# One order and one buffer table in place of another, in a hybrid encoder layer on one core

## The chip, the cores and the metric

The kernel runs on one core of a Trainium2 chip. The metric is the device time of one execution in microseconds; the median of three executions is compared. The core has five engines with a queue each: TensorE (PE, with its weight loads shown apart as PEld), VectorE (DVE), ScalarE (ACT), GpSimd (POOL) and SyncE (SP), which only issues DMAs. SP, ACT and POOL each can start DMAs. An engine does its queue in order; engines wait for one another by semaphores.

## The reference

One layer takes x (1 x 512 x 1024, float32) through a mixing step and a feed-forward step:

```python
h = rmsnorm(x, mix_norm[l])
p = h @ w_in[l]                      # 1024 x 9248: rx, ry, qkv, z, ba, gates
y_rnn = rglru_branch(rx, ry, ...) @ w_rnn_proj[l]
y_dn = deltanet_branch(qkv, z, ba, ...) @ w_dn_proj[l]
g_rnn, g_dn = jnp.split(jax.nn.sigmoid(gates), 2, axis=-1)
x = x + (g_rnn * y_rnn + g_dn * y_dn) @ w_out[l]
gt, up = jnp.split(rmsnorm(x, ffn_norm[l]) @ w_gate_up[l], 2, axis=-1)
x = x + (jax.nn.silu(gt) * up) @ w_down[l]
```

The DeltaNet branch has 8 heads, each run forwards and backwards over the sequence in chunks of 64. Within a chunk a triangular system is solved; from chunk to chunk a 128 x 128 state S is carried, and this recurrence is serial:

```python
def step(S, inp):
    v_new = u_c - w_c @ S
    o = qg_c @ S + att_c @ v_new
    S = S * exp(gl_c) + kd_c.T @ v_new
```

## The kernel before

**Stages.** x is normalised and transposed into `hh` and `hl`, its high and low parts for TensorE; a float32 product is made of three matmuls of such parts (`mm3`, L806), and the large weight matrices go through blocks of seven products in place of eight (`products` L1327, `merged` L1289, `gate_up` L1772). In order of time: the projections and the 12 blocks of the recurrent branch (`rg_front` L913, `rg_out` L951); the z products and the gate products; four DeltaNet groups of two heads each (`dn_front` L970, `dn_mats` L1014, `dn_inverse` L1051, `dn_state` L1135, `dn_out` L1214); the output projection; 22 blocks of gate and up, and down.

**The groups.** A group's `dn_mats` writes a tile `na` of which there is one, so groups follow each other. While a group runs, the z and gate products and the next group's front stand between its instructions, on TensorE above all: they are the only other work there, and the text calls them filler.

**The recurrence.** `dn_state` (L1135) works on four chains at once (two directions, two heads), in four steps, each of which takes two of the reference's chunks. Each chain owns 128 of the 512 columns of a tile. Cut to the chain of work:

```python
for ch in chains:                                                   # L1151
    T.matmul(pks[:, sl4[ch]], kq[...], st[:, sl4[ch]], ...)
for ch in chains:                                                   # L1157
    V.scalar_tensor_tensor(rhs[:, sl4[ch]], pks[:, sl4[ch]], negc[...], vn[...], ...)
for ch in chains: T.matmul(py[:, sl4[ch]], Y[...], rhs[:, sl4[ch]], ...)
A.copy(ys, py)
for ch in chains: T.matmul(pu[:, sl4[ch]], kd[:, sl4[ch]], ys[:, sl4[ch]], ...)
for ch in chains:                                                   # L1183
    V.scalar_tensor_tensor(nst[:, sl4[ch]], st[:, sl4[ch]], egl[...], pu[:, sl4[ch]], ...)
```

`kd` is made by GpSimd ahead of time. In step 0 `pks` is left out and ScalarE copies `pu`; the last step leaves out `pu`. Beside the chain, `pq` (the state with q) and `pi` (the attention with `ys`) take four matmuls each, and small operations of VectorE and ScalarE add them into the output `o`. Where a matmul writes into a PSUM tile and another engine reads any slice of that tile, the one waits for the other if it stands behind it: the dependence is kept for the tile, not for the slice.

**What sets the order.** The functions don't run their operations; `Rec` (L514) records each of them, 9344 in all, with its engine and the tiles it names. `Plan.emit` (L491) then issues them by the table `ORDER` (L31), a permutation of their numbers that was written out beforehand. So every instruction in a profile has line L525, the line in `Rec` that records it, and is told apart by its tiles. A second table, `HOMES` (L430), gives every tile of three pools (`t2`, of 512 columns, `t4`, of 1024, and `ps`, the eight PSUM banks) the buffer it lies in. A tile's first writer waits for the last users of the buffer's tile before; `Plan.emit` adds those waits.

**The start.** SP loads x in four pieces and the first weights in halves; GpSimd loads the small parameters (conv weights, biases, lambda and the norm's gain) as rows of one tile, `prow` (L719 to L733), which TensorE turns into `par`. GpSimd also does eight subtractions that split the first weights into parts.

Of the kernel before, what the change touches and what calls it, by code (L numbers as in the profile page):

```python
# [31 lines left out]
2 1686 0 1 5 6 12 14 4 1685 140 3 10 11 13 1703 7 153 152 151 17 18 19 20 21 66 67 145 142 141 5682 146 144 22 23 24  # L32
25 26 27 28 29 30 31 32 57 1704 1689 49 15 1687 65 35 33 70 43 16 143 41 71 1690 1688 1724 34 37 36 39 68 69 72 38
1705 42 73 75 40 74 59 1723 154 147 45 46 44 77 51 1707 47 97 9 58 50 60 1691 1692 1693 1697 1698 1699 1700 1701
1702 48 76 78 79 88 81 80 1706 1708 84 93 1741 85 364 1694 1742 92 52 155 55 56 1725 1727 148 53 104 1743 61 54 1726
1728 89 105 106 96 1744 1745 1715 1716 1695 1696 1709 1710 1711 1717 1718 1719 1720 1729 1730 1735 312 62 63 1712
107 1731 1736 149 150 1737 1713 1714 1721 94 64 203 98 1732 1733 86 99 1738 1739 1740 1753 1754 1755 125 95 82 1734
1747 1748 1749 117 234 100 101 909 87 90 1111 102 103 111 390 135 83 1746 1750 1751 1756 1757 1758 133 158 636 127
91 313 1752 126 134 235 124 128 109 285 363 108 1759 130 119 118 236 286 156 110 132 112 665 114 131 315 910 113 122
115 753 1080 129 1722 116 314 316 317 318 319 320 120 136 418 391 159 121 1763 883 321 322 137 855 237 754 1764 138  # L40
123 1765 582 756 1112 139 238 239 240 241 392 323 757 160 1113 762 767 1760 1761 417 324 325 326 327 528 242 243 244
245 246 247 248 249 250 251 252 253 254 255 256 257 258 259 260 261 262 263 264 265 666 328 329 330 287 393 394 331
332 333 334 335 336 337 338 339 340 341 342 343 344 345 346 637 347 348 349 350 351 352 353 354 355 356 357 358 359
360 361 362 367 266 267 268 269 270 271 272 273 274 275 276 277 278 279 280 281 282 283 284 289 368 4823 290 161 162
163 164 758 760 474 365 369 291 288 205 165 166 167 168 169 170 370 1021 292 171 172 173 174 175 176 177 178 179 180
181 182 183 184 185 186 187 188 189 190 191 192 1081 856 395 396 397 398 193 195 583 197 638 196 194 198 199 157 371
293 294 399 419 1235 400 401 402 403 404 405 406 407 858 408 409 420 410 411 412 413 414 415 1766 416 882 303 216
859 529 200 366 204 759 860 206 861 531 532 857 421 207 295 422 299 300 208 307 423 304 305 862 863 381 301 372 382
308 209 309 296 297 864 302 377 424 425 584 210 306 383 426 378 379 384 1762 212 865 1022 866 439 440 211 755 441
213 530 373 374 375 380 310 777 214 427 376 867 8 215 778 992 1173 780 311 442 298 428 431 432 429 433 434 435 436  # L50
437 763 438 385 386 387 388 781 761 218 533 534 535 536 430 786 791 219 782 783 1236 1237 784 764 868 869 870 884
785 389 475 537 538 539 1174 443 871 872 873 874 875 876 877 878 879 880 881 449 1114 451 1082 540 541 542 543 544
886 768 770 444 477 1115 772 545 546 547 548 549 887 779 888 453 765 217 501 885 550 551 552 553 554 559 4822 452
454 911 445 1116 792 794 936 560 448 1117 476 796 1118 1119 450 462 561 889 1083 1084 1085 1086 1087 1088 1089 1090
1091 1092 1175 787 789 1093 1094 1095 1096 1097 1098 1099 1100 1101 1102 1103 1104 788 790 562 468 456 502 769 771
1120 1121 1122 1123 1124 1125 1126 1127 1128 1129 1130 1131 1132 1133 1134 1135 1136 1137 1138 555 556 609 610 766
585 586 587 588 589 590 591 592 593 594 595 596 597 598 599 600 601 602 463 1139 1238 1239 1240 478 446 890 900 904
464 1140 1141 563 1105 1106 447 455 896 603 892 891 897 905 604 605 1107 898 1241 1242 901 793 899 1055 902 564 906
907 893 894 895 1054 1068 1243 469 606 607 608 613 1244 479 480 481 482 483 484 485 486 1024 466 1108 1023 829 465
557 201 1025 487 488 489 490 491 492 493 494 495 496 497 498 499 500 1109 1056 457 1110 558 1057 1245 1246 1247 1248  # L60
1249 614 615 616 565 505 506 507 569 1026 1027 1028 797 798 1250 1251 1252 1253 1254 1255 1256 508 566 570 1257 1258
611 612 567 617 631 618 619 1069 1259 1260 1261 1029 1030 1266 632 993 571 572 509 202 458 667 1031 1032 1033 568
937 620 621 1034 1035 1036 470 1037 573 574 575 1038 503 577 578 579 1039 576 903 580 622 510 1040 1041 1042 1043
1044 623 624 459 1045 801 802 625 626 1046 994 511 1047 504 731 633 803 732 1346 523 515 4788 512 513 514 467 516
517 518 728 471 627 628 629 630 938 634 472 1262 912 913 581 724 726 635 524 730 727 734 795 460 1373 1176 1177 1263
908 1070 723 939 1071 828 914 915 916 917 1178 1179 1264 725 1265 995 996 918 919 920 921 922 923 924 925 926 927
928 929 930 931 932 933 934 935 940 941 942 943 963 525 729 733 804 805 806 747 807 808 809 810 811 812 813 814 815
816 817 818 819 748 820 821 822 823 824 825 826 827 1180 1181 1182 1183 1184 1185 1186 1187 1188 1189 1190 1191 832
833 834 835 1192 1142 741 1193 1194 461 1072 735 997 1195 800 1073 4838 4856 4824 998 999 1000 1001 944 945 1002
1003 773 775 742 519 520 521 1269 668 4839 1004 1005 1006 1007 1008 1009 1010 1011 1012 958 946 1013 1048 1014 1015  # L70
947 954 749 959 1143 743 522 1204 960 736 4789 774 1196 1197 1198 1199 1200 1016 1017 1018 961 4804 955 956 745 639
744 830 831 957 962 526 1454 836 837 1374 1201 669 670 671 672 673 674 675 676 677 678 679 680 681 682 683 684 950
1455 527 951 952 776 1656 685 1205 953 948 949 1059 1058 1061 1202 640 641 1145 686 687 688 689 690 691 1144 964
1203 737 738 739 842 473 1019 1401 1206 642 643 644 645 1400 692 646 647 648 649 650 651 652 653 654 655 656 657 658
659 660 661 662 663 846 847 850 843 838 848 1281 849 751 220 844 222 224 839 840 841 851 852 853 845 1273 740 1319
1481 1279 1207 1208 1209 1210 1051 1280 694 746 750 854 4840 1050 1060 1146 1211 1212 1213 1214 1215 1216 1217 1218
1219 1220 1221 1222 1053 4805 1223 1224 1225 1226 1227 1228 1229 1230 1231 1052 1147 1148 1149 1150 1151 1152 1153
1154 4825 4841 693 1427 664 1074 1285 966 967 968 969 1272 1375 965 228 227 229 1232 1233 1270 695 696 1155 1156
1234 1062 1157 1158 1159 1160 1161 1162 1163 1164 1165 1166 1167 1168 1169 1170 970 971 972 973 232 231 233 1271
1274 223 221 974 975 976 977 978 979 980 981 982 983 1320 984 1171 985 986 987 4861 988 989 1347 1268 1172 4895 1267  # L80
1275 752 4857 1321 1322 1283 1323 990 1020 1063 1456 1298 1049 1276 230 2374 2400 2375 2379 2378 2377 1075 1287 1296
2401 1299 1303 1402 1300 1324 1325 1326 1327 1328 1329 1330 1331 1332 1333 1334 2376 1335 1336 1376 1377 1282 1378
1337 1076 1077 225 1403 1286 1338 1339 1340 1064 1066 1341 1348 1342 1343 1344 1277 1284 1345 1302 1379 1380 1381
1382 1383 1384 1385 1386 1387 1388 1389 1390 1391 1392 1393 1394 1395 1396 1350 1351 1352 4790 1065 1397 1398 1399
1278 2367 2368 2370 2371 2369 1404 1405 1428 2372 1406 1407 4806 697 698 699 700 701 702 703 704 1353 705 706 707
708 709 710 711 712 713 714 715 716 717 1657 718 719 1408 720 4791 1430 991 1431 4874 4875 721 1297 1414 1418 1409
1410 1411 1412 4807 1415 1419 1420 1354 1422 1423 1413 2373 1424 1416 4934 1301 1421 1355 1067 4792 4793 4794 4795
4796 4797 4798 4799 4800 4801 1572 1429 1417 1573 4878 4947 1425 1078 1432 1433 1434 1435 1436 1437 1438 1439 1440
1441 1442 1443 1444 1586 1445 1446 1447 2393 1448 1449 1450 722 1457 1451 1452 4876 4877 1453 1458 4802 4803 4814
# [1925 lines left out]
```

## Time and profile before

| | |
|---|---|
| median of three executions | 1127.9 us (1127.46 to 1131.09) |
| the profiled execution | 1131.04 us, its span 1129.3 us |
| PE busy | 1068.6 us, 95% |
| VectorE, ScalarE, GpSimd busy | 956.8, 764.9 and 118.8 us |
| mean PE clock granted | 0.975 |
| moved by DMA | 186.31 MB, 165 GB/s |

The span runs from the first to the last instruction that the profiler saw; the execution's time holds 1.7 us beside it. Names of tiles stand without their numbers in the profile: `ps` is any PSUM tile, `t` any tile of `t2` and `t4`, `negc`, `ge` and `par` constant tiles. An entry such as "PE ps <- DVE t: 8.7, 15, 1.8" says that PE was idle for 8.7 us, 15 times and at most 1.8 us, before instructions that write `ps`, until VectorE had written a `t`; what VectorE read before that isn't in it.

### The profile page before, as it was taken

The numbers are of one execution on the slowest core, as the hardware profiler recorded it, in microseconds if no ns is written. First come the engines' busy times: TensorE is split into PE (matmuls) and PEld (weight loads), VectorE is DVE, ScalarE is ACT, GpSimd is POOL, SyncE is SP. The second block draws the span as 40 slices with busy tenths as digits, with TensorE's granted clock in tenths as the row PEclk, the third lists the DMA queues.
The fourth block names the chain that finished last, engine by engine and source line by source line (L and its number), as shares of the span: only waits on it lengthen the run. The fifth ranks groups of instructions, "written<-read, shape, count | busy, mean of one in ns | idle before, by whom it ended". The sixth has DMA issues, their size and how long they took to land.

```text
span 1129.3 us, 18175 instructions
## 1 busy us (share of the span) xinstructions
PE 1068.6 (95%) x6623; PEld 913.1 (81%) x6623; DVE 956.8 (85%) x1707; ACT 764.9 (68%) x1397; POOL 118.8 (11%) x165
## 2 busy tenths in 40 slices
PE   7899999999999889988988898899999999999997
PEld 6887888878888668767866676788999999998786
DVE  4899999888798679847984884799989989999997
ACT  5899999974766457867986465468745554555674
POOL 5000001220302222121222000000000000000000
PEclk8999999999999999989988998999999999999999
DMA  9742472896569869964954550485154556435632
GB/s 281 199 136 91 140 190 65 198 230 180 155 182 204 180 210 259 247 150 134 236 136 92 141 177 20 168 261 178 57 169 150 162 173 202 135 109 172 214 140 75
DMA packets 170874, 186.31 MB, mean 165 GB/s; under 512 B 8704, under 2 KB 120464, under 8 KB 170784
## 3 DMA queue, kind: packets, MB, share of 16 engines
q1 hardware_dynamic: 157648, 156.43, 44.8%
q0 software_dynamic: 11808, 25.30, 13.2%
q10 hardware_dynamic: 1328, 3.42, 0.8%
q8 instruction: 52, 0.85, 0.3%
q14 instruction: 38, 0.31, 0.1%
HBM read 159.92 MB, written 18.91 MB: 158 GB/s over the span
## 4 chain that ended last, share of the span: by engine, by line
PE 72%; DVE 12%; ACT 10%; issue 3%; DMA 2%; SPq 0%; ACTq 0%; DVEq 0%
PE ps L525 72%; DVE t L525 11%; ACT t L525 7%; ACT L525 1%; DVE na L525 1%; DMA osums<-t 1%; DMA t<-in_w_in_dram 1%; ACT na L525 0%; DMA sums<-t 0%; ACT ps L525 0%; DMA t<-in_w_gate_up_dram 0%; ACT hh L525 0%; ACT rst L525 0%; SPq L525 0%; ACTq L525 0%
## 5 line engine op out<-in xcount | busy, mean ns | idle before, releaser
L525 PE MATMUL ps<-t,t 128*128 128x512 f32 (+3 forms) x3195 | 599.4, 334 | 27.5 <-DVE t L525 20.2
L525 DVE TENSOR_TENSOR t<-t,t 128x512 fp32r<-128x512 f32 (+15 forms) x839 | 553.0, 686 | 58.5 <-ACT t L525 28.2
L525 PEld LDWEIGHTS ps<-t,t 128*128 128x128 f32 (+1 forms) x3195 | 465.1, 182 | 106.4 <-DVE t L525 32.9
L525 ACT CAST t<-t 128x512 fp32r<-128x512 f32 (+2 forms) x418 | 323.0, 809 | 156.5 <-DVE t L525 66.8
L525 PE MATMUL ps<-hh,t 128*128 128x512 f32 (+2 forms) x1424 | 375.8, 341 | 0.8 <-DVE na L525 0.8
L525 PEld LDWEIGHTS ps<-hh,t 128*128 128x128 f32 (+1 forms) x1424 | 249.6, 190 | 32.4 <-ACT t L525 2.0
L525 PE MATMUL ps<-hl,t 128*128 128x512 f32 (+2 forms) x720 | 232.7, 340 | 0.0
L525 PEld LDWEIGHTS ps<-hl,t 128*128 128x128 f32 (+1 forms) x720 | 135.5, 190 | 14.0
L525 ACT COPY t<-ps 128x256 f32<-128x256 f32 (+3 forms) x168 | 70.1, 434 | 92.4 <-PE ps L525 84.9
L525 ACT ACT_TABLE_LOAD x69 | 88.5, 1283 | 4.1 <-DVE t L525 1.8
L525 DVE SCALAR_TENSOR_TENSOR t<-ps,par,t 128x511 f32<-128x511 f32 (+1 forms) x108 | 79.3, 745 | 6.5 <-ACT t L525 4.9
L525 ACT ACTIVATE t<-t 128x512 f32<-128x512 f32 (+5 forms) x118 | 72.1, 618 | 12.9 <-DVE t L525 12.2
L525 DVE TENSOR_TENSOR t<-ps,t 128x256 f32<-128x256 f32 (+1 forms) x102 | 53.3, 530 | 17.2 <-PE ps L525 14.7
L525 PE MATMUL ps<-t,na 128*128 128x128 f32 (+2 forms) x640 | 56.3, 241 | 9.8 <-DVE t L525 7.1
L525 PEld LDWEIGHTS ps<-t,na 128*128 128x128 f32 (+2 forms) x640 | 48.4, 151 | 18.3 <-DVE t L525 10.3
L525 PE MATMUL ps<-ident,t 128*128 128x128 f32 (+2 forms) x232 | 44.5, 284 | 10.6 <-DVE t L525 3.9
L525 DVE TENSOR_TENSOR t<-t 128x512 f32<-128x512 f32 (+1 forms) x84 | 53.2, 639 | 1.4 <-DMA t<-in_w_down_dram 0.8
L525 ACT ACTIVATE t<-ps,par 128x512 f32<-128x512 f32 x68 | 45.6, 710 | 7.1 <-PE ps L525 6.9
L525 POOL DMA_DIRECT2D t<-in_w_in_dram x24 | 29.8, 1303 | 194.1 <-PE ps L525 110.2
L525 PEld LDWEIGHTS ps<-ident,t 128*128 128x128 f32 (+2 forms) x232 | 30.1, 146 | 19.9 <-DVE t L525 5.7
L525 POOL TENSOR_SCALAR_AFFINE_SELECT t<-t 128x512 f32<-128x512 f32 x32 | 24.9, 787 | 138.0 <-DMA t<-gcr 85.0
L525 DVE SCALAR_TENSOR_TENSOR t<-ps,negc,t 128x128 f32<-128x128 f32 x48 | 16.4, 349 | 25.3 <-PE ps L525 25.1
(153 smaller groups left out, 700.8 us busy)
## 6 DMA issues: line engine op xcount, KB each, us to landing
t<-in_w_in_dram SPq DMA_DIRECT2D x66, 512.0 KB, 5.5
t<-in_w_gate_up_dram SPq DMA_DIRECT2D x44, 512.0 KB, 4.6
t<-in_w_in_dram POOLq DMA_DIRECT2D x24, 512.0 KB, 7.5
t<-xqd SPq DMA_DIRECT2D x48, 256.0 KB, 4.0
t<-in_w_down_dram SPq DMA_DIRECT2D x22, 512.0 KB, 3.9
t<-in_w_down_dram SPq DMA_DIRECT2D x33, 256.0 KB, 4.1
t<-in_w_in_dram SPq DMA_DIRECT2D x24, 256.0 KB, 4.6
t<-t POOLq DMA_DIRECT2D x12, 512.0 KB, 6.0
```

The costliest lines, as they stand in the source:

```text
L525: self.plan.ops.append((self.eng, {x.tensor.name for x in aps}, outs, lambda: real(*a, **kw)))
```

## The change

The code is the same in both kernels from L473 on, and so are the operations. The two tables are new: `ORDER` issues the same 9344 operations in another sequence, and `HOMES` deals the buffers out anew. A line or two of the tables, since their rows say nothing by themselves:

```diff
 ORDER = """
-2 1686 0 1 5 6 12 14 4 1685 140 3 10 11 13 1703 7 153 152 151 17 18 19 20 21 66 67 145 142 141 5682 146 144 22 23 24
...
```

What it does is seen in the engines' queues. Three places follow.

**PE, step 1 of the recurrence of the last group.** `ps1167` is `pks` (its matmuls take the state t21165), t21168 is `rhs`, `ps1169` is `py`; `ps945`, `ps946`, `ps1016` and `ps1166` belong to filler, transposes and the output of step 0. Before:

```order
L525 MATMUL ps1167_1244<-t21165_1242,t41033_1110 128x128 [waits Activation_49]
L525 MATMUL ps1167_1244<-t21165_1242,t41020_1097 128x128
L525 MATMUL ps945_1022<-t4951_1028,t4932_1009 128x512
L525 MATMUL ps946_1023<-t4951_1028,t4931_1008 128x512
L525 MATMUL ps1167_1244<-t21165_1242,t41033_1110 128x128 [waits DVE_49]
L525 MATMUL ps1167_1244<-t21165_1242,t41020_1097 128x128 [waits DVE_49]
L525 MATMUL ps1166_1243<-t21162_1239,na1136_1213 128x128 [waits Activation_49]
L525 MATMUL ps1169_1246<-t21168_1245,na1136_1213 128x128 x2
L525 MATMUL ps1169_1246<-t21168_1245,na1136_1213 128x128 [waits DVE_49]
```

With the change:

```order
L525 MATMUL ps1167_1244<-t21165_1242,t41033_1110 128x128 [waits Activation_49]
L525 MATMUL ps1167_1244<-t21165_1242,t41033_1110 128x128
L525 MATMUL ps1167_1244<-t21165_1242,t41020_1097 128x128 x2
L525 MATMUL ps1016_1093<-ident1_78,t4979_1056 128x128
L525 MATMUL ps945_1022<-t4951_1028,t4931_1008 128x512
L525 MATMUL ps1166_1243<-t21162_1239,na1136_1213 128x128 [waits Activation_49]
L525 MATMUL ps945_1022<-t4952_1029,t4931_1008 128x512
L525 MATMUL ps1169_1246<-t21168_1245,na1136_1213 128x128 [waits DVE_49] x4
```

The third and fourth matmul of `pks` each waited for VectorE; now the four stand together with one wait, and a transpose and two 512-column matmuls stand behind them, ahead of `py`.

**VectorE, the same step.** t21173 is `nst`, the new state, and ps1172 is `pu`. Before:

```order
L525 SCALAR_TENSOR_TENSOR t21168_1245<-ps1167_1244,negc97_174,t41019_1096 128x128
L525 TENSOR_SCALAR nq1053_1130<-nq1053_1130 128x8
L525 SCALAR_TENSOR_TENSOR t21168_1245<-ps1167_1244,negc97_174,t41019_1096 128x128 x3
L525 TENSOR_TENSOR t41273_1350<-t41269_1346,t41272_1349 128x1024
L525 TENSOR_TENSOR t41218_1295<-t41216_1293,t41217_1294 128x1024
L525 SCALAR_TENSOR_TENSOR t21173_1250<-t21165_1242,ge96_173,ps1172_1249 128x128 x3
```

With the change:

```order
L525 SCALAR_TENSOR_TENSOR t21168_1245<-ps1167_1244,negc97_174,t41019_1096 128x128 x4
L525 TENSOR_TENSOR t4105_182<-t4105_182,t21067_1144 128x512
L525 TENSOR_TENSOR t41273_1350<-t41269_1346,t41272_1349 128x1024
L525 SCALAR_TENSOR_TENSOR t21173_1250<-t21165_1242,ge96_173,ps1172_1249 128x128 x3
L525 SCALAR_TENSOR_TENSOR t21177_1254<-ps1176_1253,negc97_174,t41019_1096 128x128 x2
```

The reads stand in one piece; between `rhs` and `nst` stand two other operations of VectorE, as before.

**GpSimd, the start.** t266 is `prow`, and the TENSOR_TENSOR rows are the eight subtractions. Before:

```order
L525 DMA t266_143<-in_dn_norm_dram 1x16x8
L525 DMA t266_143<-in_rg_conv_b_dram 12x128
L525 DMA t266_143<-in_rg_conv_w_dram 48x128
L525 DMA t266_143<-in_dn_conv_w_dram 96x128
L525 DMA t266_143<-in_rg_bx_dram 24x128
L525 DMA t266_143<-in_rg_ba_dram 24x128
L525 TENSOR_TENSOR t4454_531<-t4452_529,t4453_530 128x512 x2
L525 DMA t266_143<-in_rg_lambda_dram 24x128
```

With the change:

```order
L525 DMA t266_143<-in_rg_ba_dram 24x128
L525 TENSOR_TENSOR t4454_531<-t4452_529,t4453_530 128x512 x2
L525 TENSOR_TENSOR t4457_534<-t4455_532,t4456_533 128x512 x2
L525 TENSOR_TENSOR t4462_539<-t4460_537,t4461_538 128x512 x2
L525 TENSOR_TENSOR t4465_542<-t4463_540,t4464_541 128x512 x2
L525 MEMSET zero_t70_147 128x1
L525 DMA t266_143<-in_rg_bx_dram 24x128
L525 AFFINE_SELECT sl5_82<-ones6_83 128x128
L525 DMA t266_143<-in_rg_lambda_dram 24x128
```

All but one of the parameter loads have moved behind the eight subtractions. On SP the first two weight halves now stand ahead of the first piece of x, and the small weights of `ba` come earlier.

875 rows, old and new, of tables (HOMES, ORDER) are left out of this document.

## The prediction

> **What bounds the kernel now.** I read the page first, for the engine that ends last. The rows are the span, the busy times, and PE's busy tenths and clock in 40 slices of 28.2 us.
>
> ```profile
> span 1129.3 us, 18175 instructions
> PE 1068.6 (95%) x6623; PEld 913.1 (81%) x6623; DVE 956.8 (85%) x1707; ACT 764.9 (68%) x1397; POOL 118.8 (11%) x165
> PE   7899999999999889988988898899999999999997
> PEclk8999999999999999989988998999999999999999
> ```
>
> TensorE is the bound, and what can be won without taking matmuls away is small: 1129.3 - 1068.6 = 60.7 us of idle, and the cycles that the throttle withheld. The eights stand in slices 14-15, 18-19, 21-23 and 25-26, so I cut the span there, at the stages of the DeltaNet groups (columns: window, its length, busy time of PE, PEld, DVE, ACT, POOL with counts, PE clock, DMA share, GB/s).
>
> ```profile
> core 0: us, PE busy (x) PEld busy (x) DVE busy (x) ACT busy (x) POOL busy (x), PEclk, DMA share, GB/s
> 0.00:56.00 56.00, 46.37 (x267) 40.74 (x268) 37.34 (x76) 37.96 (x72) 17.19 (x29) 0.91 0.85 239
> 56.00:357.00 301.00, 299.85 (x1528) 243.00 (x1527) 273.47 (x388) 254.94 (x377) 38.92 (x41) 1.00 0.61 159
> 357.00:417.50 60.50, 51.65 (x280) 42.34 (x279) 40.09 (x78) 32.24 (x73) 11.78 (x15) 1.00 0.75 185
> 491.00:535.00 44.00, 37.61 (x215) 31.96 (x215) 29.59 (x65) 29.17 (x67) 7.59 (x18) 0.92 0.43 122
> 577.00:595.80 18.80, 16.13 (x246) 12.81 (x247) 13.04 (x24) 12.51 (x27) 5.53 (x5) 0.74 0.66 148
> 595.80:636.00 40.20, 30.94 (x187) 24.66 (x186) 22.92 (x64) 19.39 (x44) 6.08 (x14) 0.95 0.44 99
> 681.20:718.20 37.00, 29.52 (x166) 23.78 (x166) 20.41 (x52) 17.26 (x44) 0.00 (x0) 0.90 0.11 36
> 745.00:1129.30 384.30, 374.13 (x2542) 346.04 (x2540) 358.10 (x577) 227.51 (x419) 0.00 (x0) 0.99 0.49 155
> ```
>
> From 56 to 357 us PE idles 1.15 us of 301, and from 745 on 10.2 of 384: nothing is to be had there. The four recurrences (`dn_state`, at 357, 491, 596 and 681 us) idle 8.85 + 6.39 + 9.26 + 7.48 = 32.0 us, the start 9.6. In the recurrences no engine is full: in the last one PE stands at 80%, DVE at 55%, ACT at 47%, DMA at 0.11. That is a chain of short steps. What ends PE's waits: first the whole span, then the windows 374 to 417.5, 491 to 535, 595.8 to 636 and 681.2 to 718.2 in that order (columns: us, times, longest).
>
> ```profile
> PEld ps L525 <- DVE t L525: 49.4, 76, 3.2
> PE ps L525 <- DVE t L525: 31.2, 52, 2.9
> ...
> PE ps L525 <- DVE t L525: 8.7, 15, 1.8
> ...
> PE ps L525 <- DVE t L525: 5.7, 10, 1.4
> ...
> PE ps L525 <- DVE t L525: 3.1, 7, 0.7
> ...
> PE ps L525 <- DVE t L525: 7.3, 15, 1.1
> ```
>
> Of PE's 31.2 us of waits on a VectorE result, 8.7 + 5.7 + 3.1 + 7.3 = 24.8 us, in 47 waits (0.53 us each), lie in the four recurrences. What such a wait is, the timeline at 496 us shows (start, duration, work, and in brackets the idle time before it and who ended it).
>
> ```profile
> 496.14 0.35 DVE L525 SCALAR_TENSOR_TENSOR t<-ps,negc,t 128x128 f32<-128x128 f32 x1 [0.25 <-PE ps L525]
> 496.55 0.49 PE L525 MATMUL ps<-t,t 128*128 128x128 f32 x2 [0.44 <-DVE t L525]
> ...
> 497.08 0.35 DVE L525 SCALAR_TENSOR_TENSOR t<-ps,negc,t 128x128 f32<-128x128 f32 x1 [0.58 <-PE ps L525]
> ...
> 498.01 0.35 DVE L525 SCALAR_TENSOR_TENSOR t<-ps,negc,t 128x128 f32<-128x128 f32 x1 [0.58 <-PE ps L525]
> ...
> 498.94 0.35 DVE L525 SCALAR_TENSOR_TENSOR t<-ps,negc,t 128x128 f32<-128x128 f32 x1 [0.58 <-PE ps L525]
> ```
>
> The four matmuls of `pks` go into four slices of one PSUM tile, each read by one scalar_tensor_tensor into `rhs`. They need nothing of each other. Yet matmul and read alternate, 0.93 us from read to read: the next matmul starts only when the read of the slice before has ended, since that read stands ahead of it in the table and the dependence is kept for the tile as a whole. The same kernel, at step 3 of group 2, also has the other order, and beside it PE's pace where nothing waits.
>
> ```profile
> 618.41 0.61 PE L525 MATMUL ps<-t,t 128*128 128x128 f32 x4
> ...
> 618.86 0.83 PE L525 MATMUL ps<-t,na 128*128 128x128 f32 x6
> ...
> 621.36 0.61 PE L525 MATMUL ps<-t,t 128*128 128x128 f32 x4
> ...
> 622.08 0.35 DVE L525 SCALAR_TENSOR_TENSOR t<-ps,negc,t 128x128 f32<-128x128 f32 x1 [1.08 <-PE ps L525]
> ...
> 622.80 0.86 DVE L525 SCALAR_TENSOR_TENSOR t<-ps,negc,t 128x128 f32<-128x128 f32 x3
> ```
>
> Four matmuls in a row start 0.11 us apart (618.41 to 618.86). First matmul to last read is 622.80 + 0.86 - 621.36 = 2.30 us here. In the alternating form it is the 0.53 us from matmul to read (496.55 to 497.08) and the reads' 498.94 + 0.35 - 496.14 = 3.15, together 3.68. Three alternations cost 1.38 us, 0.46 each.
>
> **The change, step by step.** I counted, in both orders, the places where a matmul into a tile of `dn_state` comes behind a read of another slice of it.
>
> *`pks` and `pu`*, which are the chain: 46 such places before (by group 15, 12, 6 and 13), 13 after (3, 4, 2 and 4). 33 x 0.46 = 15.2 us. Bounds: above, a read at full pace costs 0.86 / 3 = 0.29 of the 0.93, so 33 x 0.64 = 21.1; below, half is covered by matmuls of other stages that fill the gap already, 7.6.
>
> *`pi` and `pq`*, the outputs: 34 places before, 20 after. Nobody on the chain waits for them, but their matmuls hold PE's queue. 14 x 0.53 = 7.4 at most, 0 at least; I take half, 3.7.
>
> *Filler.* Of the 32.0 us of idle, 32.0 - 24.8 = 7.2 are waits for something else (ScalarE's copy of `py`, the tile `na`). The new order puts a 512-column matmul or a transpose at most of these places. Half, 3.6; bounds 0 and 7.2.
>
> *`dn_inverse`, `dn_mats`, `merged`.* The same count falls from 5 to 1 in the inverse, and rises from 4 to 8 in `dn_mats` and from 13 to 17 in the gate products: -4 + 8 = 4 waits more, 4 x 0.53 = 2.1 us lost; bounds 0 and 4.2.
>
> *Clock.* In the three later windows it was 0.92, 0.95 and 0.90. Their busy times at full clock would be shorter by 37.61 x 0.08 + 30.94 x 0.05 + 29.52 x 0.10 = 7.5 us. Half, 3.8; bounds 0 and 7.5. [...]
>
> *The start.* x's loads, the first half weights and GpSimd's queue change places.
>
> ```profile
> 3.66 0.53 POOL L525 DMA_DIRECT2D t<-in_rg_conv_w_dram  x1
> ...
> 5.74 1.28 POOL L525 TENSOR_TENSOR t<-t,t 128x512 fp32r<-128x512 f32 x1
> ...
> 8.25 0.77 PE L525 MATMUL ps<-ident,t 128*128 128x128 f32 x5 [0.85 <-DMA t<-in_x_dram]
> ...
> 13.46 0.90 PE L525 MATMUL ps<-ident,t 128*128 128x128 f32 x3 [2.94 <-DVE t L525]
> ```
>
> The wait of 2.94 us at 13.46 is again a transpose behind a read of its own tile, and there are 3 such places in `raw_transpose` before, none after; the wait for x is 0.85. Together 3.8, less what the parameters may cost. GpSimd issued six of their loads (0.53 each) ahead of its eight subtracts (1.28 each); now one stands ahead and the rest behind, so the last is issued at least 8 x 1.28 + 7 x 0.53 = 14 us after the first subtract. The first convolution needs them, and PE has matmuls of the first products until then, so I set it at 0, at most 7 (the seven issues, 3.7, and about as long again to land). The start: 3.8, bounds -3 and 7.
>
> The weight loads on SP (390 queue rows now, 396 before) are dealt out anew as well; I take 0, and the rival below is about that. **Sum:** 15.2 + 3.7 + 3.6 - 2.1 + 3.8 + 3.8 = 28.0 us. Against the profiled execution's own time, 1131.0 us (span 1129.3 and 1.7 around it), that is 1103.0. This execution was 3.1 us above the median of the three shown (1127.9), and the wait pattern I price repeats in every execution: 1127.9 - 28.0 = 1099.9. By a second way, the last recurrence alone: its work at full pace, from these rows of 681.2 to 718.2 us and a full stretch of 512-column work,
>
> ```profile
> L525 PE MATMUL ps<-t,t 128*128 128x128 f32 x72 | 14.1, 306 | 5.9 <-DVE t L525 5.9
> L525 PE MATMUL ps<-t,na 128*128 128x128 f32 x64 | 12.3, 320 | 1.6 <-DVE t L525 1.4
> L525 PE MATMUL ps<-t,t 128*128 128x512 f32 x22 | 10.6, 518 | 0.0
> L525 PE MATMUL ps<-ident,t 128*128 128x128 f32 x8 | 2.0, 355 | 0.0
> ...
> 56.47:84.70 28.23, 28.23 (x127) 23.28 (x126) 27.98 (x47) 28.07 (x43) 0.00 (x0) 1.00 0.44 136
> ```
>
> is 144 x 0.11 + 22 x 0.22 = 20.7 us in a window of 37.0. So 16.3 us are lost in this one, more than twice its idle time of 7.48, because "busy" holds each lone matmul's latency. This makes me lean to the larger side of the first term: I forecast **1099 us**.
>
> The orders of PE and VectorE at this recurrence's step 1 show that the places counted are really gone for `pks`, and one is left in `pu`.
>
> **Rivals.** *Full recovery.* The chain falls below PE's work in all four groups, and PE's own pace sets the stage. Then all 24.8 + 7.2 = 32.0 us of idle and 7.5 of clock go, and the start's 7: 1127.9 - 46.5 = 1081.4, say 1083. For it: 16.3 of 37.0 us lost in the last group. Against: each step still has py, ScalarE's copy and pu in series, and 13 + 20 places are left.
>
> *The stall only moves.* `py` needs the reads, ScalarE's copy needs all of `py`, and what is saved at `pks` is waited for at `pu`. Then the lower bounds hold: 7.6 + 0 + 0 - 2.1 + 0 + 3.8 = 9.3, 1118.6. For it: the first read now comes 0.72 us after the first matmul (621.36 to 622.08) where it came 0.53 after. Against: reads are done 1.38 us sooner in the pair of rows above.
>
> *Slower: weights late in the full stretches.* The place is SP's queue, in order, with the loads
>
> ```profile
> t<-in_w_in_dram SPq DMA_DIRECT2D x66, 512.0 KB, 5.5
> t<-in_w_gate_up_dram SPq DMA_DIRECT2D x44, 512.0 KB, 4.6
> ```
>
> A load into a buffer still in use blocks all loads behind it, and both tables, order and buffers, are new. PE has 1.15 us of slack in 56 to 357 us, and VectorE is at 91% there; so lateness goes straight into the end. These 110 loads turn the gain of 28 around from 0.25 us of mean lateness each; at 0.3 us it is 33 us, 1133. Against: the buffers let the loads run ahead by more than their 5 us today, or PE would idle more than 1.15 us in a stretch of 301.
>
> *It does not do what it says:* other stages' matmuls cover the waits that go, and the time stays at 1128. Against it stand the 24.8 us, which are PE's own idle time.
>
> **How the numbers follow.** The forecast's case has 0.56, with 1088 to 1112 as its own range (the clock, the filler and half of the first term either way); full recovery 0.20; the moved stall 0.14; late weights 0.06; no effect 0.04. The range 1080 to 1120 takes in the first three. A change of this kernel can be told from none at about 0.3%, 3.4 us: faster 0.56 + 0.20 + 0.14 = 0.90, within it 0.04, slower 0.06.
>
> **What would show it.** Right: in the four recurrences the matmul-read alternation at 0.93 us is gone from the timeline, PE's waits on VectorE there fall from 24.8 us to under 12, and their windows shrink by 4 to 9 us each, while 56 to 357 and the end keep their lengths. Wrong: the windows shrink but waits on ScalarE's copy or on `na` take their place (the moved stall); PE waits for a weight load anywhere in the full stretches; the first convolution waits for GpSimd's parameters at 25 to 35 us. A clock still at 0.90 with fewer waits would show that term wrong.

## The result, and the profile after

The changed kernel takes 1064.3 us (median of four, 1061.3 to 1065.7), the kernel before beside it 1128.3: a ratio of 0.9425, with a 95% interval of 0.9398 to 0.9451. The direction was forecast; the size was not. 64 us were won where 28 were forecast, and 1064.3 lies below the range's 1080.

The page of the changed kernel, the same rows as were shown of the kernel before:

```profile
span 1062.0 us, 18192 instructions
PE 1037.3 (98%) x6623; PEld 897.1 (84%) x6623; DVE 948.1 (89%) x1707; ACT 758.2 (71%) x1392; POOL 124.9 (12%) x165
PE   8899999999999999999999999999999999999997
PEclk9999999999999999989999999999999999999999
```

The span is shorter by 67.3 us. PE's idle time fell from 60.7 to 24.7, by 36.0; PE's busy time fell by 31.3, with the same 6623 matmuls. That second half is what the forecast's sum hardly had in it. The mean clock rose from 0.975 to 0.994: what the throttle withheld fell from 1129.3 x 0.025 = 28.2 us to 1062.0 x 0.006 = 6.4, a bound of 21.8 us for its share. Single executions of the kernel before read from 0.973 to 0.989 in the later sets, mostly 0.98, so 16 us is the more usual share.

The stages, now the whole span (columns as in the table of windows before), the recurrences at 351, 476, 562 and 631 us:

```profile
core 0: us, PE busy (x) PEld busy (x) DVE busy (x) ACT busy (x) POOL busy (x), PEclk, DMA share, GB/s
0.00:62.00 62.00, 53.80 (x315) 46.76 (x316) 47.41 (x93) 47.78 (x86) 21.12 (x29) 0.97 0.88 250
62.00:351.00 289.00, 287.49 (x1471) 233.44 (x1470) 257.85 (x365) 239.00 (x355) 35.67 (x39) 1.00 0.60 158
351.00:402.00 51.00, 50.16 (x291) 43.17 (x290) 43.04 (x84) 35.11 (x73) 11.42 (x10) 1.00 0.87 207
402.00:476.50 74.50, 71.64 (x507) 57.94 (x506) 60.68 (x129) 56.31 (x120) 26.06 (x36) 0.97 0.98 259
476.50:507.50 31.00, 31.00 (x210) 27.96 (x209) 26.19 (x63) 26.70 (x65) 5.34 (x13) 0.97 0.45 118
507.50:562.50 55.00, 53.63 (x435) 42.77 (x433) 52.71 (x136) 48.14 (x109) 15.91 (x19) 1.00 0.86 221
562.50:591.00 28.50, 28.09 (x200) 25.29 (x201) 24.71 (x67) 20.24 (x47) 7.08 (x15) 1.00 0.68 157
591.00:631.00 40.00, 39.41 (x366) 32.02 (x366) 37.26 (x107) 30.13 (x62) 2.30 (x4) 1.00 0.61 185
631.00:651.50 20.50, 20.50 (x159) 19.12 (x159) 16.08 (x42) 14.24 (x33) 0.00 (x0) 1.00 0.15 48
651.50:1062.00 410.50, 401.58 (x2685) 368.62 (x2683) 382.21 (x630) 240.58 (x450) 0.00 (x0) 1.00 0.52 162
```

The stages of the kernel before that the prediction's table does not show:

```profile
417.50:491.00 73.50, 71.26 (x507) 57.03 (x506) 59.67 (x130) 54.62 (x115) 19.60 (x28) 0.95 0.98 253
535.00:577.00 42.00, 40.52 (x183) 32.55 (x182) 39.64 (x109) 39.53 (x85) 9.84 (x12) 1.00 0.81 205
636.00:681.20 45.20, 44.17 (x380) 36.29 (x379) 37.71 (x106) 27.96 (x62) 2.31 (x4) 0.93 0.55 158
718.20:745.00 26.80, 26.42 (x137) 21.93 (x136) 24.78 (x46) 11.78 (x20) 0.00 (x0) 1.00 0.72 233
```

In the four recurrences PE now idles 0.84 + 0 + 0.41 + 0 = 1.3 us, where it idled 32.0. The last one has gone from 37.0 us to 20.5 with about as many matmul records (166 and 159). At the prediction's pace these are now 142 x 0.11 + 17 x 0.22 = 19.4 us of work.

The windows of the recurrences shrank by 9.5, 13.0, 11.7 and 16.5 us, 50.7 together, where the prediction expected 4 to 9 each. Only 30.7 of this is idle time. The other 20.0 is PE's busy time, which fell from 149.7 to 129.7 us there with 848 and 860 matmul records. The stretch ahead of the first recurrence is 6.0 us shorter (351 against 357, with 1786 and 1795 matmul records), the stretches between the recurrences lost 10.0 us together (179.5 to 169.5), and what follows the last one 0.6 (411.1 to 410.5). So 16.6 us of the 67.3 were won outside the recurrences.

PE's waits in the whole span:

```profile
PE ps L525 <- ACT t L525: 7.9, 13, 1.3
PEld ps L525 <- DVE t L525: 7.4, 19, 0.8
PE ps L525 <- DMA dtb<-in_dn_dt_bias_dram: 4.3, 1, 4.3
PE ps L525 <- DVE t L525: 1.4, 4, 0.5
```

PE's waits on a VectorE result were 31.2 us in 52; now they are 1.4 in 4. There is one new wait, of 4.3 us at the start. Step 1 of the last recurrence in the timeline shows what a step has become:

```profile
635.17 1.15 PE L525 MATMUL ps<-t,t 128*128 128x128 f32 x8
...
636.19 0.47 PE L525 MATMUL ps<-t,t 128*128 128x512 f32 x1
...
636.36 1.13 DVE L525 SCALAR_TENSOR_TENSOR t<-ps,negc,t 128x128 f32<-128x128 f32 x4
...
636.64 0.48 PE L525 MATMUL ps<-t,t 128*128 128x512 f32 x1
...
636.96 1.07 PE L525 MATMUL ps<-t,na 128*128 128x128 f32 x8
```

A float32 matmul of 128 columns stands in the trace as two, so x8 are the four of `pks`. They take 1.15 us, the four reads run in one piece of 1.13 right behind, and under them PE has filler, without a bracket of idle time anywhere, until `py` at 636.96; the last read ends at 636.36 + 1.13 = 637.49.

### The profile page after: what moved, and what is told of

It is laid out like the page before. It is cut to its first block, busy times and chain, and to the rows that moved or that the text cites. A ratio compares the mean times of both kernels' runs of the same rounds, so it can differ in the third digit from the quotient of the medians.

```text
span 1062.0 us, 18192 instructions
## 1 busy us (share of the span) xinstructions
PE 1037.3 (98%) x6623; PEld 897.1 (84%) x6623; DVE 948.1 (89%) x1707; ACT 758.2 (71%) x1392; POOL 124.9 (12%) x165
## 5 line engine op out<-in xcount | busy, mean ns | idle before, releaser
L525 DVE TENSOR_TENSOR t<-t,t 128x512 fp32r<-128x512 f32 (+18 forms) x839 | 551.4, 684 | 47.4 <-ACT t L525 30.0
L525 PE MATMUL ps<-t,t 128*128 128x512 f32 (+3 forms) x3195 | 575.1, 329 | 4.4 <-ACT t L525 3.4
L525 PEld LDWEIGHTS ps<-t,t 128*128 128x128 f32 (+1 forms) x3195 | 454.3, 180 | 74.8 <-ACT t L525 10.1
L525 ACT ACTIVATE t<-t 128x128 f32<-128x128 f32 (+5 forms) x118 | 72.2, 619 | 11.1 <-DVE t L525 9.6
L525 PE MATMUL ps<-t,na 128*128 128x128 f32 (+2 forms) x640 | 52.6, 235 | 2.2 <-ACT na L525 1.2
L525 ACT ACTIVATE t<-ps 128x256 f32<-128x256 f32 (+1 forms) x46 | 22.0, 485 | 16.4 <-PE ps L525 15.2
```

The costliest lines, as they stand in the source:

```text
L525: self.plan.ops.append((self.eng, {x.tensor.name for x in aps}, outs, lambda: real(*a, **kw)))
```

## The experiments

All of them compute the whole output. A "place" is a read of a PSUM tile with a matmul as the next operation on the same tile, counted in the order: in `dn_state` there are 88 before (28 in `pks`, 18 in `pu`, 27 in `pi`, 15 in `pq`) and 34 after (7, 6, 15, 6). The prediction counted matmuls that wait, 80 and 33, which is nearly the same. Times are medians; a difference to the changed kernel is to 1064.3, which a later set of runs gave again as 1063.6. For short, the theories are: A, the places carry the gain; E, the filler's place does. "Filler in the gaps" is counted too: PE's matmuls and transposes of other stages that stand between the last matmul of `pks`, `py` or `pu` and the first of the next of these. There are 162 before and 142 in the change.

### Matmuls first in the kernel before

`pks` and `pu` of the kernel before, in PE's queue at step 1 of the last group (`pks` is ps_1244):

```diff
 L525 MATMUL ps_1244<-t_1242,t_1097 128x128
+L525 MATMUL ps_1244<-t_1242,t_1110 128x128
+L525 MATMUL ps_1244<-t_1242,t_1097 128x128
 L525 MATMUL ps_1022<-t_1028,t_1009 128x512
 L525 MATMUL ps_1023<-t_1028,t_1008 128x512
-L525 MATMUL ps_1244<-t_1242,t_1110 128x128
-L525 MATMUL ps_1244<-t_1242,t_1097 128x128
```

> The kernel before, its buffers and all its other order kept, with one thing of the change: in dn_state the matmuls into pks and pu are drawn together and the reads come behind the last of them (46 read-then-matmul places become 5). Theory A (these places carry the gain, each delaying the whole chain behind it and not just itself): 25 to 35 us faster, about 1098. The prediction's price of 0.46 us a place: 19 us, 1109. Theory B (the gain comes from where the filler stands and from the other stages): under 8 us, over 1120.

1111.1 us, ratio 0.9851 (0.9816 to 0.9887): 16 us, 0.40 for each of 41 places. This is near the prediction's price, and far from A's.

The same for `pi` and `pq` as well:

```diff
-L525 MATMUL ps_1252<-t_1247,na_1213 128x128
+L525 MATMUL ps_1252<-t_1247,na_1213 128x128 x4
 L525 MATMUL ps_1020<-t_1029,t_1008 128x512
-L525 MATMUL ps_1252<-t_1247,na_1213 128x128
```

> As the run with pks and pu drawn together, and the same for the output tiles pi and pq (42 places more become 1). Theory A: 40 to 48 us faster than before, about 1084, since pi and pq stand in PE's queue ahead of the next step's matmuls and so on the chain too. The prediction's prices (15.2 + 3.7, a little more for the places that the change itself left): about 1105. Theory B: over 1115.

1102.1 us, 0.9762 (0.9712 to 0.9811): 25 us for 82 places, 0.31 each, again the prediction's price, not A's. Drawn together, these matmuls leave no lack of filler: 189 stand in the gaps.

### The places put back into the changed kernel

`pks` and `pu`, the reads standing where they stood in the kernel before:

```diff
-L525 MATMUL ps_1244<-t_1242,t_1110 128x128 x2
-L525 MATMUL ps_1244<-t_1242,t_1097 128x128 x2
+L525 MATMUL ps_1244<-t_1242,t_1110 128x128
+L525 MATMUL ps_1244<-t_1242,t_1097 128x128
 L525 MATMUL ps_1093<-ident_78,t_1056 128x128
 L525 MATMUL ps_1022<-t_1028,t_1008 128x512
+L525 MATMUL ps_1244<-t_1242,t_1110 128x128
 L525 MATMUL ps_1243<-t_1239,na_1213 128x128
```

> The changed kernel with 44 read-then-matmul places put back into pks and pu (13 stand there in the change), the same reads ahead of the same matmuls as in the kernel before, filler and buffers as in the change. Theory A: 25 to 35 us slower than the change, about 1094. The prediction's price: 31 x 0.46 = 14 us, 1078. Theory B: under 6 us, below 1070.

1084.1 us: 20 us for 31 places, 0.64 each, between the prediction's price and theory A's 25 to 35.

`pi` and `pq` alone (`pq` of group 2 left as in the change):

```diff
-L525 MATMUL ps_1252<-t_1247,na_1213 128x128 x2
+L525 MATMUL ps_1252<-t_1247,na_1213 128x128
 L525 MATMUL ps_1253<-t_1250,t_1110 128x128
 L525 MATMUL ps_1253<-t_1250,t_1097 128x128
 L525 MATMUL ps_1249<-t_1247,t_1248 128x128
 L525 MATMUL ps_1252<-t_1247,na_1213 128x128
-L525 MATMUL ps_1252<-t_1247,na_1213 128x128
+L525 MATMUL ps_1252<-t_1247,na_1213 128x128 x2
```

> The changed kernel with read-then-matmul places put back into the output tiles pi and pq alone (21 become 51; 42 in the kernel before), pks and pu as in the change. From the two runs before, chain alone +20 us and all four kinds +46 us. Theory C (the output tiles' waits cost as much as the chain's since they block PE's queue for chain and filler alike): +22 to +28 us, about 1089. Theory D (they cost only where the chain waits already, the two kinds meet): under +15 us, below 1079. The prediction's price, half of 0.53 us a place: +8 us, 1072.

1088.5 us: 24 us for 30 places, 0.81 each. This is theory C: in this order the output tiles, for which nobody on the chain waits, cost more than the chain's own. The change itself took away 21 such places, 42 to 21, which at 0.81 would be 17 us.

Both kinds at once, 61 places more than in the change:

> The changed kernel with the places put back in all four kinds of tile (95 in all; 88 in the kernel before, 34 in the change), filler and buffers as in the change. Theory A: 40 to 48 us slower than the change, about 1108, and the windows of the recurrences as long as before (g3 from 20 back to 35 us). The prediction's prices: 1064 + 14 + 4 = 1082. Theory B: below 1075.

1110.3 us: 46 us, about the 20 and 24 together. The last recurrence and PE's waits in this kernel:

```profile
659.40:697.00 37.60, 28.45 (x164) 21.96 (x164) 18.97 (x48) 15.46 (x38) 0.00 (x0) 0.95 0.17 58
...
PE ps L525 <- DVE t L525: 23.6, 50, 0.9
```

The window is 37.6 us long, as it was before the change (37.0), with the change's filler and buffers. So in the change's order theory A holds: its gain in the recurrences needs the matmuls to be first. One thing comes with the places and can't be told from them here: the filler that stood between `pks` and `py` now stands between single matmuls of `pks`, and in that gap 3 are left of 26. The 17 us that this kernel still gains on the one before are about what the stages outside the recurrences won (16.6).

### The filler moved on by one gap

In the changed kernel, matmuls and transposes of other stages that stood on PE between `pks`, `py` and `pu` (ps_1244, ps_1246, ps_1249) go behind the later one. That is where the next gap begins, so most of this filler moves on by one gap, and what stood inside a tile moves into the gap behind it:

```diff
 L525 MATMUL ps_1244<-t_1242,t_1097 128x128 x2
+L525 MATMUL ps_1021<-t_1028,t_1008 128x512
+L525 MATMUL ps_1243<-t_1239,na_1213 128x128
+L525 MATMUL ps_1246<-t_1245,na_1213 128x128 x4
 L525 MATMUL ps_1093<-ident_78,t_1056 128x128
 L525 MATMUL ps_1022<-t_1028,t_1008 128x512
-L525 MATMUL ps_1243<-t_1239,na_1213 128x128
 L525 MATMUL ps_1022<-t_1029,t_1008 128x512
-L525 MATMUL ps_1246<-t_1245,na_1213 128x128 x4
```

> The changed kernel with matmuls first as there, but the filler taken out of the gaps: in the four recurrences every matmul and transpose of another stage that stood on PE between pks, py and pu, or inside one of them, now stands behind the later of the two (221 matmuls of some 1,100 in these stretches; 13 and 21 read-then-matmul places as before). Theory E (what the drawing together wins only counts because filler stands in the gaps that it leaves: some 1.1 us for the reads of pks, 0.7 for ScalarE's copy, 1.1 for the reads of pu, eleven gaps in a group): 20 to 35 us slower than the change, about 1090. Theory F (the drawing together alone shortens the chain, and the filler's place is of no account): under 8 us slower.

1097.9 us: 34 us slower than the change, with the places as in the change. PE's waits:

```profile
PE ps L525 <- ACT t L525: 18.6, 26, 3.0
PE ps L525 <- DVE t L525: 11.1, 20, 1.7
```

They are 7.9 and 1.4 in the change: 20.4 us more that PE waits for ScalarE and VectorE. Theory F falls: the filler's place counts, and with the matmuls first it is worth up to 34 us.

The gaps aren't bare in this run, though. They hold 157 pieces of filler, against 142 in the change: 57 (26) between `pks` and `py`, 55 (83) between `py` and `pu`, 45 (33) between `pu` and `pks`. What is bare here and wasn't is the gap of step 0 in the last three groups, in which ScalarE copies `py`: it held 5, 5 and 6, and PE now waits 0.68, 0.76 and 0.75 us there for ScalarE. That is theory E's reason at work in three places; it doesn't account for 34 us, and no run took the filler away altogether.

### Matmuls first in the other small tiles too

The kernel before with matmuls first in `dn_state`, and the same in `dn_front`, `dn_inverse`, `dn_mats` and the transposes of x, where there were 23 more places. At the start, in PE's queue:

```diff
 L525 MATMUL ps_102<-ident_78,t_88 128x128 x2
+L525 MATMUL ps_102<-ident_78,t_90 128x128 x2
 L525 MATMUL ps_103<-ident_78,t_88 128x128 x2
-L525 MATMUL ps_102<-ident_78,t_90 128x128 x2
-L525 MATMUL ps_103<-ident_78,t_90 128x128
+L525 MATMUL ps_103<-ident_78,t_90 128x128 x2
```

> The kernel before with matmuls ahead of reads in dn_state as in the run with all four kinds of tile (1102), and the same in every other small tile: dn_front, dn_inverse, dn_mats and the transposes of x (23 places more). Theory G (what is left against the change, 38 us, is the same fault in other stages): their waits sum to about 20 us in the trace of before, so 1082 to 1088. Theory E (it is where filler stands): 1094 to 1100, most of it from the start's transposes and dn_mats.

1084.4 us, ratio 0.9631 (0.9579 to 0.9682): 18 us less than with `dn_state` alone (15 by the two ratios), as theory G had it. Its four executions have a clock of 0.991 to 0.992; with `dn_state` alone it was 0.976 to 0.989 (0.973 to 0.981 in the kernel before beside it). The stretch around the inverse of group 1, first with `dn_state` alone, then with all small tiles:

```profile
462.00:486.00 24.00, 22.21 (x285) 17.44 (x284) 13.59 (x28) 19.81 (x44) 5.47 (x6) 0.86 0.88 224
...
456.00:475.00 19.00, 18.58 (x280) 14.64 (x279) 12.97 (x26) 18.03 (x38) 5.46 (x6) 1.00 0.90 250
```

With almost the same matmuls the clock goes from 0.86 to 1.00 and the stretch from 24 to 19 us; around the next two inverses it goes from 0.86 to 0.91 and from 0.79 to 0.93. The same is seen in the tables of the kernel before and of the change, by window length times what the clock lacks to 1.00: 9.2 us were withheld in the recurrences before and 0.9 after, so of the 21.8 us that came back some 13 did so in the other stages.

### The places the change leaves, moved onto the order before

The kernel before with the order of matmuls and reads inside each small tile as in the change, exceptions included (but for 3 places more in `pu` and 2 fewer in `dn_mats`).

> The kernel before with the order of matmuls and reads of each small tile (dn_state, dn_front, dn_inverse, dn_mats, transposes of x) as in the change, exceptions included, where the run with all tiles first had no exceptions and took 1084. Theory M (drawing all together makes reads late that the next step waits for, as the 12 us in the change with all first showed; this is most of the 20 us left): 1070 to 1076. Theory E (the rest is where filler stands): 1082 to 1088 again.

1133.3 us, ratio 1.0048 (1.0029 to 1.0067): no gain at all, and both theories missed by 45 us or more. Theory M falls. PE's waits:

```profile
PE ps L525 <- DVE t L525: 24.6, 31, 3.6
PE ps L525 <- ACT t L525: 15.0, 16, 2.5
PE ps L525 <- ACT ps L525: 6.1, 6, 2.7
```

In the kernel before, the first row had 31.2 in 52, and the other two were:

```profile
PE ps L525 <- ACT t L525: 7.4, 14, 1.0
...
PE ps L525 <- ACT ps L525: 1.3, 3, 0.5
```

There are fewer waits for VectorE, but each is longer, and those for ScalarE have more than doubled. So a place has no price of its own: exceptions that cost nothing in the change hold PE in another order. That the reads come later there, against PE's position, is how I explain it; it wasn't traced read by read. What the traces do show is where the loss lies. Against the run with all tiles first, 49 us faster, the recurrences from the first read of `pks` to the last take 15 us more (99.8 against 84.4), so most of it is in the other stages; and the clock, 0.974 against 0.992, withholds some 20 us more.

### The start, and what is left in the change

GpSimd in the changed kernel idles between its subtractions, and the transposes of the parameters wait 4.3 us for its loads. First, four of the eight loads went ahead of the first subtraction and the rest in between:

```diff
 L525 DMA t266_143<-in_rg_ba_dram 24x128
+L525 DMA t266_143<-in_dn_conv_w_dram 96x128
+L525 DMA t266_143<-in_rg_lambda_dram 24x128
+L525 DMA t266_143<-in_rg_conv_w_dram 48x128
+L525 DMA t266_143<-in_rg_conv_b_dram 12x128
 L525 TENSOR_TENSOR t4454_531<-t4452_529,t4453_530 128x512 x2
```

> The changed kernel with four of GpSimd's parameter loads issued ahead of its first subtraction and the rest between the subtractions, where GpSimd idles 6.2 us; nothing else is asked for. Theory H (the transposes of the parameters at 33.9 us wait 4.29 us for the last of these loads, and PE has no other slack behind it): 3 to 5 us faster than the change, 1060. Theory I (the wait goes to the first products, whose weights the delayed subtractions make): no faster.

1066.9 us (1065.8 to 1067.2), against 1063.6 (1061.2 to 1070.5) for the change in the same set (

> The changed kernel once more, on the chip of the three runs that it is compared with: 1064, within 0.3%.

). It is no faster: theory I holds. A row of PE in this kernel's timeline:

```profile
25.55 8.67 PE L525 MATMUL ps<-t,t 128*128 128x512 f32 x26 [4.97 <-POOL t L525]
```

And of the change's:

```profile
33.89 0.43 PE L525 MATMUL ps<-ident,t 128*128 128x128 f32 x2 [4.29 <-DMA dtb<-in_dn_dt_bias_dram]
```

The wait for the loads is gone, and PE waits 4.97 us for a subtraction in its place. Then the subtractions stayed first, and behind them only the order of the rest changed:

```diff
 L525 MEMSET zero_t_147 128x1
-L525 DMA t_143<-in_rg_bx_dram 24x128
-L525 AFFINE_SELECT sl_82<-ones_83 128x128
-L525 DMA t_143<-in_rg_lambda_dram 24x128
 L525 DMA t_143<-in_rg_conv_b_dram 12x128
 L525 DMA t_143<-in_rg_conv_w_dram 48x128
 L525 DMA t_143<-in_dn_conv_w_dram 96x128
+L525 DMA t_143<-in_rg_bx_dram 24x128
+L525 DMA t_143<-in_rg_lambda_dram 24x128
+L525 DMA t_143<-in_dn_norm_dram 1x16x8
+L525 AFFINE_SELECT sl_82<-ones_83 128x128
 L525 DMA alog_149<-in_dn_a_log_dram 128x16
-L525 DMA t_143<-in_dn_norm_dram 1x16x8
```

> The changed kernel with one edit in GpSimd's queue at the start: behind the eight subtractions the six loads of parameter rows come first, and the mask sl (2.54 us there) and the load of the decay rates (0.58) behind them; everything else is the same, instruction for instruction. Theory K (the subtractions must lead, and the wait of 4.29 us at 33.9 us is for the last row load, issued at 27.0): the load is issued 3.1 us sooner, the wait falls to about 1 us, 1061. Theory L (the wait is for something else, or the next wait takes its place): 1064.

1060.0 us, ratio to before 0.9408 (0.9380 to 0.9437), the fastest of all. GpSimd in this kernel, with the last of the six loads issued at 22.63 us; in the change that was 27.03:

```profile
22.63 0.52 POOL L525 DMA_DIRECT2D t<-in_dn_norm_dram  x1
23.16 2.87 POOL L525 TENSOR_SCALAR_AFFINE_SELECT sl<-ones 128x128 f32<-128x128 f32 x1
```

PE's wait at 33.9 us is gone altogether, and only 1.5 us of waits for ScalarE came in its place (9.4 against 7.9): theory K. The change's row names another load of GpSimd's, `dtb`, as what ended that wait. It is issued right behind the last row load (27.53 us) and the transposes don't read it, so the run, and not the row, shows that the row loads were what mattered. The intervals of this kernel and of the change overlap, so that it is the faster one rests on the medians (4 us) and on the wait of the same size that is gone.

Last, the places left in the change were removed, first those in `dn_state` (34 to 7), then those of the other small tiles as well, both with the loads as in the first of the two runs on the start. In PE's queue (ps_1249 is `pu`, ps_1252 `pi`):

```diff
 L525 MATMUL ps_1252<-t_1247,na_1213 128x128
+L525 MATMUL ps_1249<-t_1247,t_1248 128x128
+L525 MATMUL ps_1252<-t_1247,na_1213 128x128 x3
 L525 MATMUL ps_1253<-t_1250,t_1110 128x128
-L525 MATMUL ps_1253<-t_1250,t_1097 128x128
-L525 MATMUL ps_1249<-t_1247,t_1248 128x128
-L525 MATMUL ps_1252<-t_1247,na_1213 128x128
```

> The same, and of the 34 read-then-matmul places left in dn_state all but 7 removed. In the trace of the change their waits sum to about 3 us, but the reads come later for it. Theory A: 2 to 5 us faster than with the parameters alone, 1057. Theory J (the change's order had put these places where nothing waits): no difference, 1060.

> The same in all the small tiles (dn_mats, dn_front, dn_inverse, the transposes of the norms too; 23 places more). Theory G: another 1 to 3 us, 1055. Theory J: 1060 or a little slower, because 3 us of dn_mats is on the chain already and the change placed its reads early on purpose.

1078.7 and 1080.3 us: 12 and 13 us slower than with the loads alone. Every theory had missed that. The runs move more than the places: the filler in the gaps is 221 and 167 pieces in them, 142 in the change. PE's waits in the first of them:

```profile
PE ps L525 <- DVE t L525: 8.5, 13, 1.0
```

They are 1.4 in 4 in the change and 1.0 in 3 with the loads alone. Its timeline in the last recurrence shows what they are (the reads with `ge` ahead of the PSUM tile make the new state, the matmuls are the next step's `pks`):

```profile
657.13 0.35 DVE L525 SCALAR_TENSOR_TENSOR t<-t,ge,ps 128x128 f32<-128x128 f32 x1 [0.61 <-PE ps L525]
657.54 0.49 PE L525 MATMUL ps<-t,t 128*128 128x128 f32 x2 [0.44 <-DVE t L525]
...
658.59 0.60 DVE L525 SCALAR_TENSOR_TENSOR t<-t,ge,ps 128x128 f32<-128x128 f32 x2
658.98 0.49 PE L525 MATMUL ps<-t,t 128*128 128x128 f32 x2 [0.96 <-DVE t L525]
```

The reads that make the state come late, and `pks` waits for each slice of it. So "matmuls first" is no rule without exception: here the exceptions that the change had kept were worth having.

## Why the prediction was wrong, point by point

**What bounds the kernel** was read rightly: the places, the four recurrences and the start. *Full recovery*, given 0.20, is the mechanism that happened: PE's own pace sets all four recurrences now. Its time, 1083, was still 19 us too long.

**The step that failed** is the price of the recurrences, which was measured by PE's idle time there: waits of about 0.5 us, and half of the idle time that was left. The sum gave them 15.2 + 3.7 + 3.6 + 3.8 = 26.3 us, and even full recovery had only their 32.0 us of idle and 7.5 of clock to win. Their windows shrank by 50.7 us, of which 20.0 had stood inside "busy". The prediction's own second way said so: 16.3 us lost in the last recurrence, where PE idled 7.48. That window did shrink by 16.5. The second way should have carried the sum for all four; it was used to lean by 1 us. Of the 20.0 us, at most 8.3 are clock. The rest is of the size of what lone matmuls cost: one alone takes 0.49 us (the row at 496.55 us), at full pace it would be 2 x 0.11 = 0.22, and 54 places fewer at 0.27 us make 14.6 us, an estimate from these rows.

The second miss is smaller. Everything outside the recurrences had 3.8 - 2.1 = 1.7 us in the sum and won 16.6.

Term by term:

- *`pks` and `pu`*, 15.2 with 21.1 as the upper bound. Put back into the change they cost 20; taken out of the kernel before they gave 16. The bounds held. The pair of rows behind the price was misread, though: x4 at 621.36 us was two matmuls of `pks` and not four, since each stands there twice. In the change the four with their reads take 637.49 - 635.17 = 2.32 us, the 2.30 of the prediction by chance.
- *`pi` and `pq`*, 3.7, bound 7.4. In the kernel before they gave 9 more when drawn together (25 less 16); put back into the change they cost 24. "Nobody on the chain waits for them" was the wrong reason for a small price. PE's queue is in order, and a matmul of `pi` that waits for VectorE holds the next step's matmuls and the filler alike: with these places put back, PE's waits on a VectorE result were 12.8 us in 24, against 1.4 in 4.
- *Filler*, 3.6, bound 7.2. Moved on by one gap, it cost 34 us. The prediction counted the idle time that other waits than the alternation caused, and not the waits that the filler already covers.
- *`dn_inverse`, `dn_mats`, `merged`*, a loss of 2.1. Drawn together in the kernel before, the other small tiles, the start's included, gave 18 us. In the change their places fall only from 23 to 18, and the stretches between the recurrences are 10.0 us shorter. The count of waits was taken for a price here as well.
- *Clock*, 3.8, bound 7.5, from three recurrence windows. There nearly all of it returned, but about two thirds of the withheld clock, 19 of 28.2 us, stood outside the recurrences. The table already had 0.74 in the inverse at 577 us (18.8 x 0.26 = 4.9 us), and the sum left it out. That half of the clock returns was my estimate, and no run shows it; over the whole span the withheld clock went from 28.2 us to 6.4. Read in pieces of half a microsecond, the clock is 0.50 or 1.00 in both traces but where it changes. Ahead of PE's last matmul it goes to 0.50 nine times in the kernel before (five times for 3.4 us, twice for 6.8, twice for 10.2) and twice in the change (3.4 and 6.8). The 0.97 from 476.5 us, where PE is busy throughout, is the end of such a stretch (0.50 up to 478.5 us, 1.00 from there); it began near 472, and PE had idled for 0.76 us ahead of 471.15. What sets one off isn't shown: in the first recurrence before the change the clock stayed at 1.00 with PE busy for 44% of 383 to 387 us.
- *The start*, 3.8. The loads' risk was there, between 0 and 7, and came out as 4.3; I took 0. What the start nonetheless won isn't measured by a run of its own; the stretch ahead of the first recurrence is 6.0 us shorter, and 3 of these are clock (56 x 0.09 = 5.0 us withheld before, 62 x 0.03 = 1.9 after).

Terms that were added as if each stood alone interact. Matmuls first are worth 25 us in the order before and 46 in the change's. Why they differ isn't shown. It isn't that filler is missing in the order before, where 189 pieces stand in the gaps; it may be how they are dealt out among the gaps, or VectorE's and ScalarE's own order, which the change also made anew.

**The rivals.** The moved stall did not come: ScalarE's waits stayed where they were (7.4 before, 7.9 after). Late weights did not come: 62 to 351 us idles 1.5 us of 289.

**What stays open.** With matmuls first in all small tiles the kernel before takes 1084, the change 1064. Of these 20 us, 13 are idle time of PE in the four recurrences (14.2 us against 1.3), and PE's waits on a VectorE result are 18.8 us against 1.4. Which part of the new order removes them was not found: no run put the change's filler, or VectorE's order, into the order before, and the attempt to split it by the exceptions failed. What the new buffer table does by itself wasn't tried, since an order and its buffers belong together.

## What to carry to other kernels

Matmuls into slices of one PSUM tile should go ahead of the first read of the tile, with other matmuls behind them to cover the reads. Here that gave 25 us in one order; undoing it cost 46 in the other, and moving the covering matmuls by one gap cost 34. Keep a read early where the next step of a serial chain waits for it, though, and don't price such a place by itself: move it in the order at hand and measure. And when a stage is bound by a chain, take its gain from its length against its matmuls at full pace, not from the idle time of the engine, since lone matmuls and a withheld clock look busy: one alone stood as 0.49 us where 0.22 is full pace, and from 709 to 712 us before the change PE was busy for 3.00 of 3.00 us at a clock of 0.50.

## What the runs showed of the hardware

In the traces of the kernel before and of the change the granted clock, read in pieces of half a microsecond, was 0.50 or 1.00 but where it changed, and ahead of PE's last matmul the stretches at 0.50 lasted 3.4, 6.8 or 10.2 us. In the kernel before, for instance, one went from 708.7 to 712.1 us in the last recurrence; from 705 to 708 PE was busy for 1.47 of 3 us. The change's 0.97 from 476.5 to 507.5 us is a mean of 2.0 us at 0.50 and 29.0 at 1.00. Nor does the mean follow PE's busy share of the same window: it was 0.86 with PE busy for 22.21 of 24.00 us around an inverse, and 1.00 in a recurrence at 51.65 of 60.50.

One AFFINE_SELECT of 128x128 on GpSimd (`sl`) took 2.87 us at 23 us in the fastest kernel. At the very start of the change GpSimd does two of that form:

```profile
1.36 0.29 POOL L525 TENSOR_SCALAR_AFFINE_SELECT loi<-ones 128x128 f32<-128x128 f32 x1
```

That is a factor of ten for the same work, and what makes it wasn't shown. The two at the start end by 1.65 us, ahead of VectorE's first operation at 1.68. In the change's two later ones, `sl` at 20.52 us (2.54) and `su` at 28.11 (0.33), VectorE is busy throughout, so that alone doesn't set the time. They end 0.16 and 0.19 us after an operation of VectorE between SBUF tiles: `sl` at 23.06 after one that ends at 22.90, `su` at 28.44 after one that ends at 28.25. No run took VectorE's work away to test it. In a queue that other engines wait for, such an operation is worth moving: with `sl` behind the row loads PE's wait of 4.29 us was gone.
